# Hybrid decoder layer on one core: gate and up products share seven PSUM accumulators, and the stage is emitted in modelled order

## The chip, the cores and the metric

The kernel runs on one core of one Trainium2 chip. The metric is the device time of one execution in microseconds (us). Traces come from one profiled execution each.

## The reference

One decoder layer on 256 tokens, all in float32, width D = 2048, hidden width D_FF = 5632. Cut to what matters here:

```python
h = rms_norm(x, g_mix); z = h @ w_in            # 2048 x 17424, feeds three token mixers
x = x + merged @ w_o                            # merged: gated sum of the mixers' outputs
h = rms_norm(x, g_ffn)
gate, up = split(h @ w_gate_up, 2, axis=-1)     # 2048 x 11264
x = x + (silu(gate) * up) @ w_down              # 5632 x 2048
x = x + (p @ w_ple) * sigmoid(rms_norm(x, g_ple) @ w_ple_gate)
return rms_norm(x, g_final)
```

The result has to be float32-accurate. The change lies in the line that makes `gate` and `up`.

## The kernel before

**A product.** The 256 tokens are two halves of 128, called h = 0 and 1. The activations, transposed, are the stationary operand (128 features by 128 tokens); a weight tile (128 features, "k tile", by 512 columns) streams past. Both operands are split into a high and a low part of type fp32r, and one product of a k tile with one half is three matmuls of 512 columns: high by high, high by low, low by high (`products`, rows L244, L245, L246). A block of 512 output columns has one PSUM accumulator (`acc`) per half.

**A weight.** Weights come in pairs of k tiles, 128x2x512 float32, 512 KB. SP issues the load into a tile `raw`; ScalarE (ACT) copies it to the high part `whi` (L110); VectorE (DVE) subtracts, `wlo = raw - whi` (L111). A pair is two L244-L246 products per half, 12 matmuls.

**The stages.** Mixers (w_in and three output projections), w_o in four blocks c = 0..3, the gate and up blocks, w_down, then the per-layer embedding (w_ple, w_ple_gate). D_FF is cut into eleven blocks j of 512. For each j there is a group of sixteen k tiles for gate (evacuated by `ev_gate`: ACT sigmoid, DVE multiply) and one for up (`ev_up`: DVE multiply, giving the tile `ga`), then `ga` is transposed on PE and split into the stationary `aT` for w_down. `CUT = 5`: gate and up for j = 0..4, a pass over w_down with what is there, gate and up for j = 5..10, a second pass. Each pass adds its four blocks into the residual `xr` (`ev_down`, two DVE adds of 128x512 per block).

**The order.** `run(plan)` cuts the groups into chunks of four k tiles and emits them in turn: loads up to three chunks ahead (`PREF_DMA = 2`), splits up to two (`PREF_SPLIT = 2`), transposes two chunks after their evacuation (`LAG = 2`). Five buffers for raw tiles, five for split pairs, five PSUM banks for accumulators, three (`misc`) for transposes. These pools are open for the whole kernel, so the first gate weights are loaded and split while w_o's matmuls still run. The normalised input of gate and up is made per block c of xr after w_o: transposes, then `scaled_split` by g_ffn (`next_stat`, tiles `xhi`, `xlo`). The tokens' norms (`rn`) are applied in the evacuation.

**The end.** The last group is the last 256 columns of w_ple_gate, kind "hold": its split weights are kept in SBUF (`whold`), half 0 of the tokens is multiplied with all sixteen k tiles first, then half 1, and `ev_last` (sigmoid `pgs`, L965, final norm, output) of half 0 runs under the matmuls of half 1.

Of the kernel before, what the change touches and what calls it, by code (L numbers as in the profile page):

```python
# [19 lines left out]
P = 128  # L20
# [20 lines left out]
class Group:  # L41
# [6 lines left out]
    def __init__(self, w, kts, c0, n, stat, evac, need=(), pre=None, kind="tok", cost=1.3):  # L48
        self.w, self.kts, self.c0, self.n = w, list(kts), c0, n
        self.stat, self.evac, self.need, self.pre, self.kind = stat, evac, need, pre, kind  # L50
        self.cost = cost
        self.ps = None
        self.held = []


class Chunk:
    def __init__(self, g, ks, first, last):
        self.g, self.ks, self.first, self.last = g, ks, first, last
        self.raw = None
        self.parts = None  # L60


@with_exitstack
def kernel(
# [80 lines left out]
    junk = const.tile([P, NB], F32, name="junk")
    siga0 = const.tile([P, 2, 248], F32, name="siga0")
# [32 lines left out]
    def split_w(c):  # L179
# [70 lines left out]
    def run(plan):  # L250
# [3 lines left out]
        while now[0] < len(chunks):  # L254
# [12 lines left out]
            if c.first:  # L267
                for name in g.need:
                    finish(name)
                g.ps = [  # L270
                    acc.tile([P, NB], F32, tag="acc", name=nm("acc")) for _ in range(2)
# [547 lines left out]
    run(plan)  # L819
# [20 lines left out]
    xr2 = [big(f"xr{c}", (P, 2, 1024)) for c in range(2)]  # L840
    xr = [col(xr2, c) for c in range(4)]
    xT = {"f": [], "p": []}
# [10 lines left out]

    def ev_wo(c):
        def f(g, i):
# [3 lines left out]
            defer(i, lambda: next_stat("f", c, "g_ffn"))  # L859
# [3 lines left out]
    for c in range(4):  # L863
        nc.gpsimd.dma_start(out=xr[c], in_=x_v[:, :, c * NB : (c + 1) * NB])
    gfb = big("gfb", (P, D))
    nc.gpsimd.dma_start(out=gfb, in_=g_final.partition_broadcast(P))
    plan = [Group(w_o_v, ks16, c * NB, NB, blk(mT), ev_wo(c)) for c in range(4)]


# [5 lines left out]
    def ev_gate(j):  # L875
        def f(g, i):
            m = med("ga")
            for h in range(2):
                act.activation(out=m[:, h, :], in_=g.ps[h], func=AF.Sigmoid, scale=rr("f", h))
                stt(m[:, h, :], g.ps[h], rr("f", h), m[:, h, :], ALU.mult, ALU.mult)  # L880
            gt[j] = m
# [3 lines left out]
    def ev_up(j):  # L885
        def f(g, i):
            m = gt[j]
            for h in range(2):
                stt(m[:, h, :], g.ps[h], rr("f", h), m[:, h, :], ALU.mult, ALU.mult)

            def later():
                a = big("aT", (P, 2, 4, T), F32R)
                aT[j] = (a[:, 0, :, :], a[:, 1, :, :])
                to_stat(m, *aT[j])

            defer(i, later)

        return f

    def ev_down(c, final):  # L900
        def f(g, i):
            for h in range(2):
                tt(xr[c][:, h, :], xr[c][:, h, :], g.ps[h], ALU.add)
            if final:
                stats_add("p", c, xr[c])
                defer(i, lambda: next_stat("p", c, "g_ple"))
# [4 lines left out]
    CUT = 5  # L911
    for lo, hi in ((0, CUT), (CUT, NJ)):
        for j in range(lo, hi):
            plan.append(Group(w_gu_v, ks16, j * NB, NB, x_stat("f"), ev_gate(j)))
            plan.append(Group(w_gu_v, ks16, NJ * NB + j * NB, NB, x_stat("f"), ev_up(j)))
        for c in range(4):
            plan.append(Group(w_dn_v, range(4 * lo, 4 * hi), c * NB, NB, blk(aT), ev_down(c, hi == NJ)))
# [4 lines left out]
    def prep_p():  # L922
# [4 lines left out]
        split(pT["hi"], pT["lo"], pt)  # L927

    def ev_ple(c):
        def f(g, i):  # L930
            m = med("ple")
            for h in range(2):
                act.activation(out=m[:, h, :], in_=g.ps[h], func=AF.Copy)
            pl[c] = m
# [3 lines left out]
    def pg_half(ps, c, h, a, n, slot):  # L938
# [8 lines left out]
        tt(xh, xh, gfb[:, c * NB + a : c * NB + a + n], ALU.mult)  # L947
# [108 lines left out]
```

## Time and profile before

| | |
|---|---|
| median of 3 runs | 1902.97 us (1901.8 to 1903.25) |
| the profiled execution | 1903.29 us, its span 1901.4 us |
| PE busy | 1884.7 us (99%), 8688 matmuls and transposes |
| DVE busy | 1187.9 us (62%), 1409 instructions |
| ACT busy | 927.1 us (49%), 1067 instructions |
| POOL busy | 9.1 us, 22 instructions |
| memory | 359.58 MB read, 190 GB/s over the span |
| mean clock of PE | 0.998 |

Busy shares are means over stages with different limits. An engine that is not the last to be waited for has idle time that costs nothing; the rows of waits and the chain of work that ended last tell which engine that is. In such rows `wlo<-raw,whi` is an instruction that writes the tile wlo from raw and whi, L111 its line, `<-ACT whi L110` what released it.

### The profile page before, as it was taken

How to read it: one execution, taken by the hardware profiler on the slowest of the kernel's cores; microseconds unless marked ns; L12 is line 12 of the kernel's file. 1: busy time of each engine (PE TensorE's matmuls, PEld its weight loads, DVE VectorE, ACT ScalarE, POOL GpSimd, SP SyncE). 2: the span in 40 equal slices, each digit the busy share in tenths (PEclk: the TensorE clock that was granted, in tenths of full speed). 3: DMA queues.
4: the chain of work that ended last, by engine and by line, in shares of the span. 5: the costliest groups of instructions: out<-in, count | busy, mean ns of one | idle time of the engine just before them, and what ended most of it. 6: DMA issues, size and time to landing. Idle time of an engine off the chain costs nothing.

```text
span 1901.4 us, 22742 instructions
## 1 busy us (share of the span) xinstructions
PE 1884.7 (99%) x8688; PEld 1570.9 (83%) x8688; DVE 1187.9 (62%) x1409; ACT 927.1 (49%) x1067; POOL 9.1 (0%) x22
## 2 busy tenths in 40 slices
PE   8999999999999999999999999999999999999998
PEld 7888888888888888888888888888888888888887
DVE  6457777668889888645555555554545555555555
ACT  6656556554444435644445544443344444444554
POOL 0000000000000000000000000000000000000000
PEclk9999999999999999999999999999999999999999
DMA  8766556556666656676655666665666666655553
GB/s 309 237 182 185 174 178 189 173 150 176 197 182 196 192 154 220 190 242 189 209 189 187 186 191 189 189 189 190 196 190 190 196 191 190 188 188 189 183 183 122
DMA packets 190254, 363.18 MB, mean 191 GB/s; under 512 B 11600, under 2 KB 20432, under 8 KB 189760
## 3 DMA queue, kind: packets, MB, share of 16 engines
q1 hardware_dynamic: 189248, 358.12, 61.6%
q0 software_dynamic: 896, 3.61, 0.6%
q8 instruction: 68, 1.11, 0.2%
q14 instruction: 42, 0.34, 0.1%
HBM read 359.58 MB, written 2.10 MB: 190 GB/s over the span
## 4 chain that ended last, share of the span: by engine, by line
PE 98%; DVE 1%; DMA 0%; ACT 0%; SPq 0%; issue 0%; DVEq 0%
PE acc L246 32%; PE acc L245 32%; PE acc L244 32%; PE tr L313 2%; PE sc L522 1%; DMA x<-in_x_feat_dram 0%; DVE rw L688 0%; DVE wlo L111 0%; PE ov L593 0%; PE ov L594 0%; PE ov L592 0%; ACT whi L110 0%; PE sc L549 0%; SPq L165 0%; SPq L164 0%; ACT hhi L321 0%
## 5 line engine op out<-in xcount | busy, mean ns | idle before, releaser
L111 DVE TENSOR_TENSOR wlo<-raw,whi 128x1024 fp32r<-128x1024 f32 (+2 forms) x678 | 813.2, 1202 | 673.6 <-ACT whi L110 672.3
L110 ACT ACTIVATE whi<-raw 128x1024 fp32r<-128x1024 f32 (+2 forms) x678 | 706.0, 1043 | 903.7 <-PE acc L246 832.3
L244 PE MATMUL acc<-whi,hhi 128*128 128x512 f32 (+1 forms) x1120 | 433.1, 387 | 5.2 <-ACT whi L110 5.1
L245 PE MATMUL acc<-wlo,hhi 128*128 128x512 f32 (+1 forms) x1120 | 430.3, 384 | 0.5 <-DVE wlo L111 0.5
L246 PE MATMUL acc<-whi,hlo 128*128 128x512 f32 (+1 forms) x1120 | 430.6, 384 | 0.0
L244 PE MATMUL acc<-whi,xhi 128*128 128x512 f32 (+1 forms) x832 | 321.4, 386 | 0.0
L246 PE MATMUL acc<-whi,xlo 128*128 128x512 f32 (+1 forms) x832 | 320.6, 385 | 0.0
L245 PE MATMUL acc<-wlo,xhi 128*128 128x512 f32 (+1 forms) x832 | 320.3, 385 | 0.0
L244 PEld LDWEIGHTS acc<-whi,hhi 128*128 128x128 f32 x1120 | 210.9, 188 | 46.2 <-ACT whi L110 5.6
L245 PEld LDWEIGHTS acc<-wlo,hhi 128*128 128x128 f32 x1120 | 210.9, 188 | 42.2 <-DVE wlo L111 1.4
L246 PEld LDWEIGHTS acc<-whi,hlo 128*128 128x128 f32 x1120 | 210.8, 188 | 41.8
L246 PEld LDWEIGHTS acc<-whi,xlo 128*128 128x128 f32 x832 | 156.3, 188 | 31.5
L244 PEld LDWEIGHTS acc<-whi,xhi 128*128 128x128 f32 x832 | 156.3, 188 | 30.9
L245 PEld LDWEIGHTS acc<-wlo,xhi 128*128 128x128 f32 x832 | 156.4, 188 | 30.8
L244 PE MATMUL acc<-whi,aT 128*128 128x512 f32 x352 | 137.5, 391 | 0.0
L246 PE MATMUL acc<-whi,aT 128*128 128x512 f32 x352 | 137.1, 389 | 0.0
L245 PE MATMUL acc<-wlo,aT 128*128 128x512 f32 x352 | 136.9, 389 | 0.0
L104 DVE SCALAR_TENSOR_TENSOR cv<-uT,vec,cv 128x255 f32<-128x255 f32 (+15 forms) x240 | 110.8, 466 | 4.8
L246 PEld LDWEIGHTS acc<-whi,aT 128*128 128x128 f32 x352 | 66.1, 188 | 13.8
L245 PEld LDWEIGHTS acc<-wlo,aT 128*128 128x128 f32 x352 | 66.1, 188 | 13.6
L244 PEld LDWEIGHTS acc<-whi,aT 128*128 128x128 f32 x352 | 66.1, 188 | 13.6
L244 PE MATMUL acc<-whi,mT 128*128 128x512 f32 x128 | 50.2, 392 | 0.0
(250 smaller groups left out, 1369.1 us busy)
## 6 DMA issues: line engine op xcount, KB each, us to landing
raw<-in_w_in_dram SPq DMA_DIRECT2D x262, 512.0 KB, 3.7
raw<-in_w_gate_up_dram SPq DMA_DIRECT2D x176, 512.0 KB, 3.7
raw<-in_w_down_dram SPq DMA_DIRECT2D x88, 512.0 KB, 4.1
raw<-in_w_gla_out_dram SPq DMA_DIRECT2D x32, 512.0 KB, 3.7
raw<-in_w_o_dram SPq DMA_DIRECT2D x32, 512.0 KB, 3.6
raw<-in_w_ple_gate_dram SPq DMA_DIRECT2D x24, 512.0 KB, 4.4
raw<-in_w_sc_out_dram SPq DMA_DIRECT2D x16, 512.0 KB, 4.3
raw<-in_w_cf_out_dram SPq DMA_DIRECT2D x16, 512.0 KB, 4.3
```

The costliest lines, as they stand in the source:

```text
L104: dve.scalar_tensor_tensor(out=o, in0=a, scalar=s, in1=b, op0=op0, op1=op1)
L110: a = act.activation(out=hi, in_=src, func=AF.Copy)
L111: b = dve.tensor_tensor(out=lo, in0=src, in1=hi.bitcast(F32), op=ALU.subtract)
L244: pe.matmul(o, lhsT=shi[:, hs], rhs=whi, start=st, stop=False)
L245: pe.matmul(o, lhsT=shi[:, hs], rhs=wlo, start=False, stop=False)
L246: pe.matmul(o, lhsT=slo[:, hs], rhs=whi, start=False, stop=sp)
L313: pe.transpose(b[:, q, h * P : h * P + P], src[:, h, (j + q) * P : (j + q) * P + P], ident,)
L522: pe.matmul(b[:, e, :], lhsT=K[:, dt, :], rhs=Q[:, dt, :], start=q == 0, stop=q == 1)
```

## The change

**Seven products instead of eight.** Gate block j and up block j are one `Quad`: per pair of k tiles a 2 by 2 by 2 block product (two halves of tokens, two k tiles, two blocks), eight products. `PAIRS = "soosooso"` names the eight pairs of k tiles. In an "s" pair (0, 3, 6) seven products of sums replace the eight: seven stationary operands are combinations of the four blocks of the input (`quad_stat`, tile `st`), and seven moving operands are taken from four pieces of weights: gate, up with gate's first k tile added in place, a sum tile (`sum`), and one more k tile. DVE makes them with four additions of 128x512; three pieces are split in full, one half. The seven go to PSUM banks 7, 6, 1, 2, 5, 3, 4.

**Eight products with five differences.** In an "o" pair there are eight products (24 matmuls) into banks 2, 4, 5, 3, which needs six stationary combinations. Gate's piece is split as before. For up's piece ACT writes `whi` and then `wlo = -whi`, and a DMA issued by POOL with `accum_op=add` adds the weight from HBM onto it. There are 55 of these accumulating DMAs, 512 KB each.

**Combining.** `quad_mid` and `quad_end` form the four outputs from the seven banks: per quad one ACT copy, seven DVE additions or subtractions with PSUM, four `stt` and two sigmoids; before there were two sigmoids per j and four multiplications.

**The order.** From gate and up to the end a class `Flow` emits the instructions: it keeps a model of when ACT, DVE and PE are free and puts splits, evacuations and transposes between the products by it. Loads are issued one by one while fewer than `RAWS = 4` raw tiles live, `PARTS = 7` split pairs. PSUM: seven banks for accumulators, one (`misc`) for transposes.

**Pools and passes.** The mixers and w_o are one plan in the old `run`. Then the pools for raw tiles, split pairs, t4 and PSUM are closed and opened with the new sizes. w_down has three passes, after j = 0..3, 4..7, 8..10. `whold` is one tile per pair of k tiles.

Where the order of instructions moves, in three places. First PE at the end of w_o. Before (`mT` is w_o's stationary, `xhi` and `xlo` that of gate and up), the last row of w_o and the first of gate:

```order
L244 MATMUL acc_8109<-whi_8198,mT_7642 128x512
L245 MATMUL acc_8109<-wlo_8199,mT_7642 128x512
L246 MATMUL acc_8109<-whi_8198,mT_7642 128x512
L244 MATMUL acc_8290<-whi_8230,xhi_7808 128x512
L245 MATMUL acc_8290<-wlo_8231,xhi_7808 128x512
L246 MATMUL acc_8290<-whi_8230,xlo_7809 128x512
```

After, at the same place (L639 to L641 are the old `products`, L236 to L238 the new `three`, `tr` a transpose, `st` the combined stationary; in brackets the semaphores that an instruction waits for):

```order
L640 MATMUL acc_8126<-wlo_8216,mT_7643 128x512
L641 MATMUL acc_8126<-whi_8215,mT_7643 128x512
L1276 MATMUL tr_8318<-ident,xr_1331_7602 128x128 [waits DMASW6_49,DVE_49]
L1276 MATMUL tr_8318<-ident,xr_1331_7602 128x128 [waits DVE_49]
L1276 MATMUL tr_8318<-ident,xr_1331_7602 128x128 x2
L236 MATMUL acc_8363<-whi_8325,st_7815 128x512 [waits DMAHW2_49,DMAHW1_49,DMAHW3_49,DMAHW0_49,DMAHW4_49,DMASW2_49,DMAHW5_49,DMASW1_49,DMAHW6_49,DMASW0_49,DMAHW7_49,Activation_49,Pool_49]
L236 MATMUL acc_8380<-whi_8325,st_7815 128x512
L237 MATMUL acc_8363<-wlo_8326,st_7815 128x512 [waits DVE_49]
```

The products follow w_o directly before and need two tiles that were split in w_o's time; now four transposes and tiles of the new pools stand in between.

Second, ACT at the same place. Before, whi_8198 is w_o's last split:

```order
L110 ACTIVATE whi_8198<-raw_8136 128x1024 [waits DMAHW7_49,PE_49]
L110 ACTIVATE whi_8230<-raw_8190 128x1024 [waits DMAHW0_49,PE_49]
L110 ACTIVATE whi_8234<-raw_8192 128x1024 [waits DMAHW1_49,PE_49]
L110 ACTIVATE whi_8282<-raw_8226 128x1024 [waits DMAHW2_49,PE_49,Activation_49]
L110 ACTIVATE whi_8286<-raw_8228 128x1024 [waits DMAHW3_49,PE_49,Activation_49]
L830 ACTIVATE junk,ssq_7755<-xr_1309_7569 128x512 [waits DMASW6_49,DVE_49]
```

After, whi_8215 is w_o's last split (L505 is the old `split`, L209 and L213 those of `split_ops`, L1224 the squares for the norm, L1260 the scaling of `quad_stat`):

```order
L505 ACTIVATE whi_8215<-raw_8153 128x1024 [waits DMAHW7_49,PE_49]
L209 ACTIVATE whi_8325<-raw_8312 128x1024 [waits DMAHW1_49,DVE_49,PE_49]
L1224 ACTIVATE junk,ssq_7756<-xr_1331_7602 128x512 [waits DMASW6_49,DVE_49]
L209 ACTIVATE whi_8331<-raw_8310 128x1024 [waits DMAHW0_49]
L1224 ACTIVATE junk,ssq_7756<-xr_1331_7602 128x512 [waits DVE_49,Activation_49]
L209 ACTIVATE whi_8338<-sum_8323 128x1024
L209 ACTIVATE whi_8346<-raw_8312 128x512 [waits DVE_49]
L696 ACT_TABLE_LOAD
L696 ACTIVATE s_8275<-v_8273 128x2 [waits DVE_49]
L1260 ACTIVATE sz_8349<-tr_8318,vec 128x2x128 [waits PE_49]
L1260 ACTIVATE sz_8349<-tr_8318,vec 128x256
L209 ACTIVATE whi_8370<-raw_8314 128x1024 [waits DMAHW2_49]
```

The splits for gate stood ahead of the squares of w_o's last block and now stand among them, and the first one's tile lies where a tile of w_o's closed pool lay: it waits for the last matmul of w_o (PE_49).

Third, PE at the end, in the hold group. Before (acc_14203 is half 0, acc_14204 half 1; rows left out in between are more of the same k tiles), where the one half passes into the other:

```order
L244 MATMUL acc_14203<-whold_14238,xhi_13241 128x256
L245 MATMUL acc_14203<-whold_14238,xhi_13241 128x256
L246 MATMUL acc_14203<-whold_14238,xlo_13242 128x256
L244 MATMUL acc_14204<-whold_14149,xhi_12759 128x256
L245 MATMUL acc_14204<-whold_14149,xhi_12759 128x256
L246 MATMUL acc_14204<-whold_14149,xlo_12760 128x256
```

After (acc_14808 is half 0, acc_14873 half 1; whold_14769 is the last of eight pairs of k tiles, whold_14742 the fifth):

```order
L236 MATMUL acc_14873<-whold_14742,xhi_13955 128x256
L236 MATMUL acc_14808<-whold_14769,xhi_13955 128x256 [waits Activation_49]
L237 MATMUL acc_14873<-whold_14742,xhi_13955 128x256
L238 MATMUL acc_14873<-whold_14742,xlo_13956 128x256
...
L237 MATMUL acc_14808<-whold_14769,xhi_13955 128x256 [waits DVE_49]
L238 MATMUL acc_14808<-whold_14769,xlo_13956 128x256
...
L238 MATMUL acc_14873<-whold_14742,xlo_13956 128x256
L236 MATMUL acc_14873<-whold_14751,xhi_13955 128x256
```

Half 1 starts before half 0 is through, and half 0 ends 19 matmuls ahead of the end where it ended 48 ahead of it.

The diff, cut to what is spoken of here:

```diff
+    def split_ops(self, piece, t, src, deps=(), load=None, frees=(), cost=1.2, sl=slice(0, 2), neg=None):
...
+        a = self._op("A", cost * 0.88, lambda: nc.scalar.activation(out=hi(), in_=src(), func=AF.Copy), deps, load, piece,
+                     frees if neg else ())
+        if neg:
+            def go():
+                nc.scalar.activation(out=lo(), in_=hi().bitcast(F32), func=AF.Copy, scale=-1.0)
+                nc.gpsimd.dma_start(out=lo(), in_=neg, accum_op=ALU.add)
...
+    BANKS = "6712453"
...
+    def add_quad(self, g):
...
+            r1, r2 = (Load(g.w, 2 * p, c, NB) for c in g.cs)
+            if kind == "s":
...
+                        self.nc.vector.tensor_tensor(out=X(0), in0=R2(0), in1=R2(1), op=ALU.add),
...
+                b1 = self.split_ops(pc[0], 0, lambda r=r1: r.raw, load=r1)
+                t1 = self.add_op(lambda R2=R2: R2(0), lambda R2=R2: R2(0), lambda R1=R1: R1(0), [t3], r1)
+                t2 = self.add_op(lambda X=X: X(1), lambda R2=R2: R2(0), lambda R2=R2: R2(1), [t1], r1)
+                self.split_ops(pc[1], 0, lambda r=r2: r.raw, [t1], r2, [r2])
+                t4 = self.add_op(lambda R1=R1: R1(0), lambda R1=R1: R1(1), lambda X=X: X(1), [t2, b1], r1)
+                self.split_ops(pc[2], 0, lambda x=x: x[0], [t2], None, [])
+                self.split_ops(pc[3], 0, lambda r=r1: r.raw[:, 0:1, :], [t4], r1, [r1], 0.65, slice(0, 1))
+                terms = [("7", 3, 2, 0), ("6", 5, 2, 1), ("1", 0, 0, 0), ("2", 1, 0, 1), ("5", 4, 1, 0), ("3", 6, 1, 1), ("4", 2, 3, 0)]
...
+                self.split_ops(pc[1], 0, lambda r=r2: r.raw, load=r2, frees=[r2],
+                               neg=g.w[:, 2 * p : 2 * p + 2, g.cs[1] : g.cs[1] + NB])
+                self.split_ops(pc[0], 0, lambda r=r1: r.raw, load=r1, frees=[r1])
+                for part, (z, slot, i) in enumerate((("2", 0, 0), ("4", 2, 0), ("5", 2, 1), ("3", 4, 1))):
...
+    PAIRS = "soosooso"
+    def quad_stat(p, b, z):
+        st = big("st", (P, 2, 8, P), F32R)
...
+            act.activation(out=o, in_=v[:, q, :, :], func=AF.Copy, scale=v1("g_ffn", 2 * p + q))
+        if PAIRS[p] == "s":
+            n = 7
+            tt(z[:, 3, :], z[:, 7, :], z[:, 0, :], ALU.subtract)
+            tt(z[:, 4, :], z[:, 7, :], z[:, 2, :], ALU.subtract)
+            tt(z[:, 5, :], z[:, 0, :], z[:, 4, :], ALU.subtract)
+            tt(z[:, 6, :], z[:, 1, :], z[:, 5, :], ALU.subtract)
+        else:
+            n = 6
+            tt(z[:, 4:6, :], z[:, 0:2, :], z[:, 2:4, :], ALU.subtract)
+        split(st[:, 0, :n, :], st[:, 1, :n, :], z[:, :n, :])
...
+    run(plan)
+    for d in deferred:
+        d[1]()
+    phase.close()
+    phase = open_pools(raws=(4,), sums=(1,), wparts=(7,), t4=(3,), at=(1,), acc=(1, PSUM), misc=(1, PSUM))
...
+    def quad_mid(g, ps):
+        g.v, g.m = v, m = med("vx"), med("ga")
+        return [
+            flow.op("A", 0.6, lambda: act.activation(out=m[:, 0, :], in_=ps["1"], func=AF.Copy)),
+            flow.op("D", 0.7, lambda: tt(v[:, 0, :], ps["6"], m[:, 0, :], ALU.subtract)),
+            flow.op("D", 0.7, lambda: tt(v[:, 1, :], v[:, 0, :], ps["7"], ALU.add)),
+        ]
...
-    CUT = 5
-    for lo, hi in ((0, CUT), (CUT, NJ)):
+    for lo, hi in ((0, 4), (4, 8), (8, NJ)):
         for j in range(lo, hi):
-            plan.append(Group(w_gu_v, ks16, j * NB, NB, x_stat("f"), ev_gate(j)))
-            plan.append(Group(w_gu_v, ks16, NJ * NB + j * NB, NB, x_stat("f"), ev_up(j)))
+            plan.append(Quad(w_gu_v, j * NB, (NJ + j) * NB, PAIRS, quad_mid, quad_end(j)))
...
-    run(plan)
+    flow.run(plan)
```

More of the change, by code (lines that the diff above doesn't have):

```diff
@@ L60, in __init__ @@
         self.parts = None
+class Quad:
+    def __init__(self, w, c0, c1, pairs, mid, end):
+        self.w, self.cs, self.pairs, self.mid, self.end = w, (c0, c1), pairs, mid, end
+        self.ps = {}
+class Op:
+    def __init__(self, eng, cost, fn, deps=()):
+        self.eng, self.cost, self.fn, self.deps = eng, cost, fn, list(deps)
+        self.end = None
+class Load:
+    def __init__(self, w, k, c0, n):
+        self.w, self.k, self.c0, self.n = w, k, c0, n
+        self.raw, self.freed = None, False
@@ L86, in nm, with open_pools @@
         return f"{s}_{uid[0]}"
+    pools = {}
+    def open_pools(**sizes):
+        stack = ExitStack()
+        for name, (bufs, *space) in sizes.items():
+            kw = dict(space=PSUM) if space else {}
+            pools[name] = stack.enter_context(tc.tile_pool(name=nm(name), bufs=bufs, **kw))
+        return stack
+    phase = open_pools(
+        gla=(1,), raws=(5,), wparts=(5,), t4=(5,), acc=(5, PSUM), misc=(3, PSUM)
+    )
     def big(name, shape=(P, 8, T), dt=F32):
@@ L270, in run @@
                 g.ps = [
-                    acc.tile([P, NB], F32, tag="acc", name=nm("acc")) for _ in range(2)
+                    pools["acc"].tile([P, NB], F32, tag="acc", name=nm("acc")) for _ in range(2)
                 ]
@@ L873, in rr @@
         return rn[key][:, h : h + 1]
[L875 to L881, printed above, removed]
-        return f
[L885 to L892, printed above, removed]
-                aT[j] = (a[:, 0, :, :], a[:, 1, :, :])
-                to_stat(m, *aT[j])
-            defer(i, later)
-        return f
+    flow = Flow(nc, tc, pools, nm, big, split, quad_parts=lambda p: fst[p])
@@ new lines, in a_stat, with pe_part, rest, x_part @@
+    def a_stat(j, m, z):
+        def pe_part(b):
+            if z == 0:
+                a = pools["at"].tile([P, 2, 4, T], F32R, tag="at", name=nm("aT")) if j % 4 == 3 else big("aT", (P, 2, 4, T), F32R)
+                aT[j] = (a[:, 0, :, :], a[:, 1, :, :])
+            four(b, m, z)
+        def rest(b):
+            split(aT[j][0][:, z : z + 2, :], aT[j][1][:, z : z + 2, :], b)
+        return pe_part, rest, 0.8, ("a", 2 * j + z // 2)
+    def x_part(c, j):
+        def pe_part(b):
+            four(b, xr[c], j)
+        def rest(b):
+            quad_stat(2 * c + j // 2, b, med("sz", (P, 8, P)))
+        return pe_part, rest, 2.0, ("f", 2 * c + j // 2)
@@ L900, in ev_down, with p_part, pe_part, rest @@
+    def p_part(c, j):
+        def pe_part(b):
+            if c % 2 == 0 and j == 0:
+                xT["p"].append((big("xhi", dt=F32R), big("xlo", dt=F32R)))
+            four(b, xr[c], j)
+        def rest(b):
+            hi, lo = xT["p"][-1]
+            for q in range(2):
+                a = (c % 2) * 4 + j + q
+                scaled_split(hi[:, a, :], lo[:, a, :], b[:, q, :], v1("g_ple", 4 * c + j + q))
+        return pe_part, rest, 1.0, ("p", 2 * c + j // 2)
     def ev_down(c, final):
-        def f(g, i):
-            for h in range(2):
-                tt(xr[c][:, h, :], xr[c][:, h, :], g.ps[h], ALU.add)
+        def f(g, ps):
+            def add(h):
+                tt(xr[c][:, h, :], xr[c][:, h, :], ps[h], ALU.add)
+            ops = [flow.op("D", 0.7, lambda h=h: add(h)) for h in range(2)]
```

449 lines of the change are left out of this document (391 added, 58 removed).

## The prediction, made before the changed kernel ran

> **What bounds the kernel now.** First the page's busy times and the chain of work that ended last, then the waits of PE over the whole span.
>
> ```profile
> PE 1884.7 (99%) x8688; PEld 1570.9 (83%) x8688; DVE 1187.9 (62%) x1409; ACT 927.1 (49%) x1067; POOL 9.1 (0%) x22
> PE 98%; DVE 1%; DMA 0%; ACT 0%; SPq 0%; issue 0%; DVEq 0%
> ```
>
> ```profile
> PE acc L244 <- ACT whi L110: 5.1, 1, 5.1
> PE mu L690 <- DVE rw L688: 1.7, 1, 1.7
> PE acc L245 <- DVE wlo L111: 0.5, 1, 0.5
> ```
>
> PE is 98% of the chain, and its waits add up to 7.3 us, one at the start and two in the mixers. So behind w_o PE never waits: what is taken from its queue there is gained in full, and what makes it wait there is lost in full. Now the stage of gate and up, from the groups of a stretch that holds the end of w_o and gate and up blocks; the windows below give the shares of a stretch of gate and up alone (columns: wall; busy us of PE, PEld, DVE, ACT, POOL; clock; DMA share; GB/s).
>
> ```profile
> L111 DVE TENSOR_TENSOR wlo<-raw,whi 128x1024 fp32r<-128x1024 f32 x77 | 94.4, 1225 | 96.2 <-ACT whi L110 96.1
> L110 ACT ACTIVATE whi<-raw 128x1024 fp32r<-128x1024 f32 x77 | 81.7, 1061 | 112.2 <-PE acc L246 112.2
> L104 DVE SCALAR_TENSOR_TENSOR ga<-acc,y,ga 128x512 f32<-128x512 f32 x16 | 11.3, 746 | 2.1 <-ACT ga L879 2.1
> L879 ACT ACTIVATE ga<-acc,y 128x512 f32<-128x512 f32 x9 | 6.1, 689 | 3.9 <-PE acc L246 3.9
> L111 DVE TENSOR_TENSOR aT<-tr,aT 128x512 fp32r<-128x512 f32 x8 | 5.1, 681 | 0.0
> L110 ACT ACTIVATE aT<-tr 128x512 fp32r<-128x512 f32 x8 | 4.3, 585 | 0.0
> L313 PE MATMUL tr<-ident,ga 128*128 128x128 f32 x32 | 4.1, 272 | 0.0
> ```
>
> ```profile
> 30.00:40.00 10.00, 10.00 (x46) 8.29 (x45) 3.97 (x5) 7.47 (x8) 0.00 (x0) 1.00 1.03 387
> 1046.00:1160.00 114.00, 114.00 (x516) 94.57 (x516) 62.61 (x68) 54.02 (x62) 0.00 (x0) 1.00 0.65 189
> ```
>
> ACT waits for PE (a buffer comes free), DVE for ACT: both have room, and DMA at 189 GB/s is well below the 387 GB/s that it reaches when full. DVE is at 55% there, ACT at 47%.
>
> **The change, step by step.** The base is the profiled execution, 1903.29 us, 0.3 us above the median of the runs (1902.97), which changes nothing at this size.
>
> 1. Matmuls. Per quad three "s" pairs take 21 matmuls instead of 24: 9 fewer, times 11 quads 99; the order of PE's instructions shows that the rest stays (8344 rows to 8245). What one costs is the spacing in the stream:
>
> ```profile
> 1319.77 0.39 PE L244 MATMUL acc<-whi,aT 128*128 128x512 f32 x1
> 1363.97 0.39 PE L244 MATMUL acc<-whi,aT 128*128 128x512 f32 x1
> ```
>
> 195 matmuls lie between these starts: 44.20/195 = 0.2267 us. Gain 99 x 0.2267 = **22.4 us**, and no more, whatever the other engines do.
>
> 2. Does a quad stay bound by PE? PE: 8 x 24 - 9 = 183 matmuls, 41.5 us. Further rows for 128x512 tiles and for the small steps:
>
> ```profile
> L101 DVE TENSOR_TENSOR xr<-xr,acc 128x512 f32<-128x512 f32 x2 | 1.3, 679 | 0.0
> L111 DVE TENSOR_TENSOR wlo<-raw,whi 128x512 fp32r<-128x512 f32 x12 | 8.2, 690 | 7.9 <-ACT whi L110 7.7
> L321 ACT ACTIVATE xhi<-tr,vec 128x256 fp32r<-128x256 f32 x6 | 2.6, 471 | 1.9 <-DVE xlo L104 1.9
> L301 ACT ACT_TABLE_LOAD x1 | 1.3, 1283 | 0.0
> L830 ACT ACTIVATE junk<-xr 128x512 f32<-128x512 f32 x2 | 1.2, 623 | 0.0
> L830 ACT ACTIVATION_READ_ACCUMULATOR junk<-xr 128x1 f32 x2 | 0.4, 185 | 0.0
> ```
>
> DVE per quad: "s" pairs 3 x (3 full subtractions x 1.225 + 0.690 + 4 additions x 0.68) = 21.3; "o" pairs 5 x 1.225 = 6.1; seven PSUM combinations x 0.68 = 4.8; four multiplications x 0.746 = 3.0; two splits of aT x 0.68 = 1.4. Sum 36.5 of 41.5 us, 88%. ACT: "s" 3 x (3 x 1.061 + 0.63) = 11.4; "o" 5 x 3 x 1.061 = 15.9; evacuation and aT 3.2. Sum 30.5, 73%. So PE stays the longest, but DVE's slack falls from some 45% to 12%. What hides all these additions is PE's own queue of products; the cover on DVE is 5.0 us per quad.
>
> 3. The accumulating DMAs, five of 512 KB per quad. The trace has no accumulating transfer. The nearest rows are the POOL queue's loads (KB, us to landing) beside SP's:
>
> ```profile
> raw<-in_w_gate_up_dram SPq DMA_DIRECT2D x176, 512.0 KB, 3.7
> xr<-in_x_dram POOLq DMA_DIRECT2D x4, 512.0 KB, 7.5
> gfb<-in_g_final_dram POOLq DMA_DIRECT2D x1, 1024.0 KB, 5.3
> pt<-in_p_feat_dram POOLq DMA_DIRECT2D x1, 256.0 KB, 3.3
> L864 POOL DMA_DIRECT2D xr<-in_x_dram x4: 722/730/762, 836.0 to 838.2; - x4
> ```
>
> Latency: four xr loads issued within 2.2 us took 7.5 us each; 256 KB alone 3.3, 1 MB alone 5.3. I take 4.5 (a plain 512 KB lies near 4, and reading what is there comes on top), ends 3.3 and 9.5 (7.5 and 2 for the second read). In mid-quad the negation is emitted some 13 us (58 to 60 matmuls) ahead of the product that reads it, of which two ACT passes take 2.1: 11 us are there, and a landing of up to 9.5 is hidden. POOL does nothing else in this stage, so its queue holds up nobody. Throughput: 512 KB at 387 GB/s is 1.35 us; with k the cost of an accumulating byte relative to a plain one a quad needs 16 x 1.35 + 5 x 1.35 k = 21.7 + 6.8 k: 28.5 us at k = 1, 35.2 at 2, 42 at 3. I take k between 1 and 2: one read more per byte written; cost nothing. The Trainium skill ("Collectives: The Full Stack", "The bandwidth ceiling: the fold count and why AG ≠ RS ≠ AR") has reduce-scatter at 32.35 GB/s against 62.28 for all-gather, since an add reads two sources, a ratio of 1.93. An estimate from that figure puts a quad's DMA at 35 us, under PE's 41.5, and the sum stays; no run here shows it.
>
> 4. The border of w_o and the first quad. Before, two splits of gate were ready when w_o ended and there was no wait. Now the new pools lie over the old ones: SP's first load waits for DVE's last w_o split, and ACT's first split for w_o's last matmul. By hand from that matmul, in ACT's order: split 1.06, two squares with read-outs 1.6, two splits 2.1 (4.8), DVE's half split behind them ends at 6.7; ACT goes on with a half split 0.63, table load 1.28, root 0.2, two scaled copies 0.94 (7.9), two splits of the first "o" pair (10.0), split of st about 0.95, negation 1.06 (12.0), accumulating DMA 4.5 (16.5), then ten matmuls, 2.3: 18.8. PE's work up to there is 45 matmuls (10.2) and 8 transposes at 4.1/32 (1.0), 11.2. Loss **7.5 us**; with the ends of the landing, 6.3 and 12.5. A gain is excluded: nothing waits there now.
>
> The longest single idle of PE in that chain is from 13.5 to 16.5, 3 us. How the clock (the column before the last two) takes idle time, the end of the trace shows, where the last matmul is at 1892:
>
> ```profile
> 1892.00:1895.00 3.00, 0.14 (x2) 0.00 (x0) 2.15 (x8) 2.16 (x4) 0.00 (x0) 0.98 0.62 209
> 1895.00:1898.00 3.00, 0.00 (x0) 0.00 (x0) 1.68 (x5) 0.72 (x1) 0.00 (x0) 0.50 0.48 178
> ```
>
> It falls to 0.50 about 3 us after the last matmul, so a landing over about 5 us would also bring slow matmuls here. The Trainium skill ("TensorE: Matmul & The Clock Gate", "Part 1: The HAM clock gate") has a window of about 3.4 us of idle before the half clock and as long busy before the full one; the trace agrees with the first. By it an estimate of 1.7 us would come on top, and the forecast would be 1895.
>
> 5. The tail. In the hold group half 0 ended 48 matmuls of 256 columns before the end, now 19.
>
> ```profile
> 1886.42 0.47 ACT L965 ACTIVATE pgs<-acc,y 128x256 f32<-128x256 f32 x1 [1.88 <-PE acc L246]
> 1890.19 0.71 ACT L988 ACTIVATE xr<-xr,fr 128x512 f32<-128x512 f32 x1
> 1892.18 0.47 ACT L965 ACTIVATE pgs<-acc,y 128x256 f32<-128x256 f32 x1 [1.28 <-PE acc L246]
> ```
>
> The two evacuations start 5.76 us apart, 0.12 per matmul; ACT is done with half 0 after 4.48 us (1890.90). With 19 x 0.12 = 2.3 us the second starts 2.2 us late. And the last three pairs' whold reuse buffers that half 1 frees only then: two or three short waits, 0.6 in all (between 0 and 2). Together **+2.8** (0 to 5).
>
> 6. The single transpose bank. A block's second four transposes wait until DVE has split the first. Before there were three banks. By hand both arrive within about a microsecond, so 0 to 1.5 us per quad; I take 0.2, nearest to "arrives in time", **+2** (0 to 16).
>
> 7. Free: the third pass over w_down (8 more additions of 0.68 on DVE, under 16 k tiles of products each), the residual's transposes moved into quads, the late load of gfb (5.3 us, needed a whole group later).
>
> Sum: 1903.29 - 22.4 + 7.5 + 2.8 + 2 = **1893** us.
>
> **The rivals.**
>
> *VectorE loses its lead.* At 88%, with additions in place that need one another (sum, then gate into up, then the next sum), the order decides. Before, DVE waited 96.2/77 = 1.25 us for ACT per split; in the chain of an "s" pair ACT and DVE take turns four times. If PE waits 0.6 us per quad more, 6.6 in all, two thirds of what is left of the gain are gone, at 0.95 us per quad all of it; at 1.9 us the time is 1914. For it: 12% of slack where there were 45. Against: seven buffers of split pairs instead of five let DVE run ahead, and by my hand chain an "s" pair's last split is ready 4 to 5 us before PE reads it. Time 1899 to 1914.
>
> *The accumulating DMAs fill the queues* (the slower side). The place is every quad's five accumulations; from k = 2.9 DMA needs as long as PE (21.7 + 19.8), and from k = 3.2 the remaining gain of 10 us is gone (0.95 per quad). At k = 4 a quad takes 48.8, 11 x 7.3 = 80 us more: 1973. For it: POOL's loads took 7.5 where SP's took 3.7, and there is no row of an accumulation. Against: that was with four at once beside SP's.
>
> *The border and the tail are hidden.* If splits and landing come early enough, items 4 to 6 shrink to 3: 1884. Against: the order shows PE's first product waiting for a split that waits for PE.
>
> That the products are not saved is excluded by the order.
>
> **How the numbers follow.** A measurement tells about 0.2%, 3.8 us, from no change: "same" is 1899.2 to 1906.8. Main case 1885 to 1899, 0.58; hidden border 0.08; VectorE 0.19, about half of it within "same", half slower; DMA 0.13; 0.02 for others. Faster 0.67, same 0.11, slower 0.22. The range takes the first three, with items 4 to 6 at their ends (1903.3 - 22.4 + 3 = 1884 to 1914), and leaves out the DMA case: 1883 to 1914. The likeliest case's own range is 1885 to 1899.
>
> **What would show it.** Right: the spacing of matmuls unchanged at 0.227; in the first 20 us behind w_o PE waits for ACT, DVE and a POOL transfer, 6 to 12 us in all; in later quads PE's waits below 0.5 us each, DVE near 88%, ACT near 73%; an accumulating DMA lands in 4 to 7 us; the two pgs stand 4.5 us apart. Wrong: waits of PE for wlo in each quad (VectorE), or a DMA share near 1.0 and raw tiles that ACT waits for (DMA), or landings over 11 us, which would turn up as a wait of PE for the queue of POOL in each "o" pair.

## The result: 1958.65 us, 2.95% slower, and the profile after

The changed kernel takes 1958.65 us (median of four runs, 1955.82 to 1962.88) against 1903.07 (four runs, 1901.8 to 1903.25); the ratio is 1.0295, interval 1.0271 to 1.032. The profiled execution has a span of 1954.1 us, 52.7 more than before. From the page of the changed kernel: busy times, the queues, the chain of work that ended last, the accumulating DMAs.

```profile
PE 1892.1 (97%) x8589; PEld 1553.9 (80%) x8589; DVE 1310.5 (67%) x1646; ACT 1041.1 (53%) x1207; POOL 75.3 (4%) x77
q0 software_dynamic: 15856, 32.44, 9.1%
PE 75%; DVE 10%; DMA 9%; issue 3%; ACT 2%; DVEq 0%; POOL 0%; SPq 0%; ACTq 0%; POOLq 0%
raw<-in_w_gate_up_dram SPq DMA_DIRECT2D x176, 512.0 KB, 4.6
wlo<-in_w_gate_up_dram POOLq DMA_DIRECT2D x55, 512.0 KB, 8.0
```

The 99 matmuls are gone (8688 records to 8589), yet the chain, 98% PE before, is 75% PE: a fifth of the span now runs through DVE and DMA. The waits of PE, and those for a raw weight tile on the two engines that make its parts (engine, waiting tile and line, releaser: us, times, longest). L236 to L238 are the three matmuls of a product; vx and ga are the tiles into which DVE combines the banks:

```profile
PE acc L236 <- DVE vx L496: 17.0, 15, 1.8
PE acc L237 <- DMA wlo<-in_w_gate_up_dram: 8.1, 1, 8.1
PE tr L1276 <- DVE aT L506: 6.0, 8, 1.6
PE tr L1276 <- DVE ga L499: 5.7, 3, 2.3
...
PE acc L237 <- DVE wlo L220: 4.2, 6, 1.5
```

```profile
ACT whi L209 <- DMA raw<-in_w_gate_up_dram: 82.5, 27, 4.9
DVE raw L228 <- DMA raw<-in_w_gate_up_dram: 65.8, 23, 4.8
DVE sum L266 <- DMA raw<-in_w_gate_up_dram: 40.4, 20, 3.9
```

The last three groups are new: in this stage of the kernel before, ACT's splits waited for PE alone. PE's waits name DVE, and DVE and ACT wait for loads. The timeline of DVE and then PE in the first quad of the second pass shows how the one becomes the other (start, length, instruction, idle before it):

```profile
1386.57 0.69 DVE L266 TENSOR_TENSOR sum<-raw 128x512 f32<-128x512 f32 x1 [2.14 <-DMA raw<-in_w_gate_up_dram]
1391.09 0.69 DVE L228 TENSOR_TENSOR raw<-raw,raw 128x512 f32<-128x512 f32 x1 [3.83 <-DMA raw<-in_w_gate_up_dram]
...
1397.69 0.68 DVE L220 TENSOR_TENSOR wlo<-raw,whi 128x512 fp32r<-128x512 f32 x1
1398.29 0.68 DVE L496 TENSOR_TENSOR vx<-acc,ga 128x512 f32<-128x512 f32 x1
...
1403.27 1.27 DVE L496 TENSOR_TENSOR vx<-vx,acc 128x512 f32<-128x512 f32 x2
```

```profile
1393.69 0.50 PE L237 MATMUL acc<-wlo,st 128*128 128x512 f32 x1 [1.49 <-DVE wlo L220]
1399.84 0.47 PE L236 MATMUL acc<-whi,st 128*128 128x512 f32 x1 [0.60 <-DVE vx L496]
1404.60 0.50 PE L236 MATMUL acc<-whi,st 128*128 128x512 f32 x1 [1.75 <-DVE vx L496]
```

DVE stands still for 2.1 and 3.8 us until a raw tile lands, then runs without a gap, and the combinations of this quad, behind the late splits in its queue, come too late for PE, which needs their banks again. The windows of the same stage (columns: wall; busy us of PE, PEld, DVE, ACT, POOL; clock; DMA share; GB/s) show a DMA share of 0.88 and a clock that drops where PE has stood:

```profile
1086.80:1093.60 6.80, 3.82 (x9) 3.05 (x10) 4.21 (x6) 1.69 (x2) 0.00 (x0) 0.50 0.99 260
1274.60:1278.00 3.40, 3.40 (x11) 2.63 (x10) 2.13 (x3) 1.54 (x2) 0.00 (x0) 0.50 0.76 251
1400.00:1440.00 40.00, 36.93 (x165) 29.80 (x165) 26.40 (x35) 23.25 (x26) 4.84 (x4) 1.00 0.88 238
```

And a part that nobody had touched is longer. The last matmul of w_o, before and after:

```profile
1059.66 0.39 PE L246 MATMUL acc<-whi,mT 128*128 128x512 f32 x1
```

```profile
1068.54 0.40 PE L641 MATMUL acc<-whi,mT 128*128 128x512 f32 x1
```

PE's order up to there is the same row for row, and so are its waits (5.2 against 5.1 us at the start, 1.7 in the mixers). A stretch of 60 us in the mixers holds fewer matmuls (PE busy and its count, clock, DMA share, GB/s; before, then after):

```profile
640.00:700.00 60.00, 60.00 (x266) 1.00 0.59 181
```

```profile
640.00:700.00 60.00, 60.00 (x264) 1.00 0.60 187
```

The starts there are 0.2289 us apart (95 between 630.333 and 652.077) where they were 0.2267.

Split by the starts of PE's matmuls, the 52.7 us of span are: 8.9 up to the end of w_o; 41.0 from there to the last product of w_down (731.98 us before, 772.97 now), in which the 99 matmuls save 22.4 and PE's gaps over the normal spacing grow from 0.7 to 64.1; 2.75 in the rest. Of the 64.1, 14.1 lie at the border of w_o (up to 1118 us) and 50 in the quads and passes behind it. PE's waits in this stage add up to 43 us; the rest is in gaps that the rows of waits do not count in full, and in matmuls at the half clock, some 7 us (an estimate: PE was busy for 14 us of the 17 in which the clock stood at 0.50).

### The profile page after: what moved, and what is told of

Its sections match the earlier page's. It is cut to its first block, busy times and chain, and to the rows that moved or that the text cites. A ratio compares the mean times of both kernels' runs of the same rounds, so it can differ in the third digit from the quotient of the medians.

```text
span 1954.1 us, 23164 instructions
## 1 busy us (share of the span) xinstructions
PE 1892.1 (97%) x8589; PEld 1553.9 (80%) x8589; DVE 1310.5 (67%) x1646; ACT 1041.1 (53%) x1207; POOL 75.3 (4%) x77
## 4 chain that ended last, share of the span: by engine, by line
PE 75%; DVE 10%; DMA 9%; issue 3%; ACT 2%; DVEq 0%; POOL 0%; SPq 0%; ACTq 0%; POOLq 0%
PE acc L639 17%; PE acc L641 17%; PE acc L640 17%; DMA raw<-in_w_gate_up_dram 7%; PE acc L237 7%; PE acc L238 7%; PE acc L236 7%; DVE wlo L220 6%; ACT whi L209 2%; DVE raw L228 1%; PE tr L708 1%; PE tr L1276 1%; DVE vx L496 1%; DMA raw<-in_w_down_dram 1%; PE sc L917 1%
## 5 line engine op out<-in xcount | busy, mean ns | idle before, releaser
L506 DVE TENSOR_TENSOR wlo<-raw,whi 128x1024 fp32r<-128x1024 f32 (+2 forms) x378 | 450.0, 1195 | 301.6 <-ACT whi L505 300.7
L505 ACT ACTIVATE whi<-raw 128x1024 fp32r<-128x1024 f32 (+2 forms) x378 | 390.7, 1036 | 472.4 <-PE acc L641 438.0
L209 ACT ACTIVATE whi<-raw 128x1024 fp32r<-128x1024 f32 (+1 forms) x333 | 329.2, 1003 | 314.4 <-PE acc L238 170.7
L639 PE MATMUL acc<-whi,hhi 128*128 128x512 f32 (+1 forms) x1120 | 436.8, 390 | 5.2 <-ACT whi L505 5.2
L220 DVE TENSOR_TENSOR wlo<-raw,whi 128x1024 fp32r<-128x1024 f32 (+1 forms) x278 | 315.8, 1142 | 180.7 <-ACT whi L209 180.4
L641 PE MATMUL acc<-whi,hlo 128*128 128x512 f32 (+1 forms) x1120 | 433.3, 387 | 0.0
L236 PE MATMUL acc<-whi,st 128*128 128x512 f32 x671 | 265.4, 397 | 16.2 <-DVE vx L496 15.9
L237 PE MATMUL acc<-wlo,st 128*128 128x512 f32 x671 | 263.9, 393 | 12.4 <-DMA wlo<-in_w_gate_up_dram 8.1
L238 PE MATMUL acc<-whi,st 128*128 128x512 f32 x671 | 261.5, 392 | 0.0
L639 PEld LDWEIGHTS acc<-whi,hhi 128*128 128x128 f32 x1120 | 211.2, 189 | 46.2 <-ACT whi L505 5.2
L641 PEld LDWEIGHTS acc<-whi,hlo 128*128 128x128 f32 x1120 | 211.0, 188 | 45.1
L236 PEld LDWEIGHTS acc<-whi,st 128*128 128x128 f32 x671 | 126.4, 189 | 50.3 <-DVE vx L496 17.2
L237 PEld LDWEIGHTS acc<-wlo,st 128*128 128x128 f32 x671 | 127.0, 189 | 41.6 <-DMA wlo<-in_w_gate_up_dram 8.9
L238 PEld LDWEIGHTS acc<-whi,st 128*128 128x128 f32 x671 | 127.0, 189 | 26.6
L236 PE MATMUL acc<-whi,aT 128*128 128x512 f32 x352 | 138.9, 395 | 2.8 <-DVE ga L496 1.7
L238 PE MATMUL acc<-whi,aT 128*128 128x512 f32 x352 | 138.5, 393 | 0.0
L214 POOL DMA_DIRECT2D wlo<-in_w_gate_up_dram x55 | 66.2, 1204 | 845.6 <-ACT wlo L213 833.9
L236 PEld LDWEIGHTS acc<-whi,aT 128*128 128x128 f32 x352 | 66.6, 189 | 17.2 <-DVE ga L496 2.1
```

Of the source, the lines that this page charges most:

```text
L209: a = self._op("A", cost * 0.88, lambda: nc.scalar.activation(out=hi(), in_=src(), func=AF.Copy), deps, load, piece, frees if neg else ())
L214: nc.gpsimd.dma_start(out=lo(), in_=neg, accum_op=ALU.add)
L220: lambda: nc.vector.tensor_tensor(out=lo(), in0=src(), in1=hi().bitcast(F32), op=ALU.subtract),
L236: pe.matmul(o, lhsT=s[0], rhs=w[0], start=start, stop=False)
L237: pe.matmul(o, lhsT=s[0], rhs=w[1], start=False, stop=False)
L238: pe.matmul(o, lhsT=s[1], rhs=w[0], start=False, stop=stop)
```

## The experiments

Theory B says that the accumulating DMAs make the loads late; theory C that the seven banks, the one transpose bank and DVE's work do it alone; theory A that the mixers are slower because their weight tiles lie elsewhere in SBUF.

**e1_align**, where the tiles lie, first try.

```diff
-    siga0 = pools["gla"].tile([P, 2, 248], F32, name="siga0")
+    siga0 = pools["gla"].tile([P, 2, 256], F32, name="siga0")[:, :, :248]
```

> One tile of the pool gla is 64 bytes longer, so that the split weight tiles of the mixers and w_o begin at a multiple of 128 bytes again; nothing else changes. Theory A (alignment: in the changed kernel these tiles begin at 64 modulo 128, and matmuls that read them start 0.2289 us apart instead of 0.2267): the end of w_o comes at 1060 us instead of 1068.5, the time falls by 8.9 us to 1950. Rival (the slow stretch belongs to that execution or chip, or to the new order of pools in another way): no change, 1958.

1971.69 us (ratio 1.0368, 1.0344 to 1.0392): the wrong way. The mixers were slower still, 260 matmuls in the same 60 us, and w_o's last matmul started at 1083.58. So 64 bytes in one tile move the end of a part that is bound by PE by 15 us; place matters, but it is not the multiple of 128.

**e5_same_offset**, second try.

```diff
+    siga0 = pools["gla"].tile([P, 2, 400], F32, name="siga0")[:, :, :248]
```

> One tile of the pool gla is 1216 bytes longer, so that the split weight tiles of the mixers begin at 1536 modulo 2048, as the stationary tiles of t8 do (before, both began at 896; in the changed kernel at 320 against 1536; with 64 bytes more at 384 against 1536, where the matmuls stood 0.2324 us apart). Theory A2 (matmuls of 512 columns are slower where moving and stationary tile differ in that offset): spacing 0.2267 and the end of w_o at 1060 us, 8.9 earlier; time about 1950. Rival A3 (the spacing depends on something else of the new order of pools): between 0.2280 and 0.2330, 1955 to 1975.

1938.97 us (1.0196, 1.0179 to 1.0213). The mixers are back to the old pace:

```profile
640.00:700.00 60.00, 60.00 (x266) 1.00 0.56 180
```

```profile
1059.17 0.39 PE L641 MATMUL acc<-whi,mT 128*128 128x512 f32 x1
```

Theory A2's number for the end of w_o held. The time fell by more than the 8.9 us of that part; the rest, some 11 us, lies in the quads (772.97 us to 761.5), where nothing was changed and the kernel's own runs differ by up to 7. By the addresses of the built program the operands of the quads lie at 1536 and 1536 modulo 2048 in both kernels, and the spacing there is 0.227 in both; what made the 11 us stays open.

**e2_no_accumulate** and **e3_plain_copy**, the DMAs themselves.

```diff
-                nc.gpsimd.dma_start(out=lo(), in_=neg, accum_op=ALU.add)
```

> Leaves out the 55 accumulating DMAs (the low part of up's weights in the pairs with eight products is then only minus the high part); ACT's negation and all else stay. Theory B (the accumulating DMAs make the loads of raw weights late, and DVE's queue, which holds the additions for the next pair ahead of the evacuations, passes that on to PE): the 10 us at the border of w_o go and most of the 45 us of waits in the quads, time 1905 to 1920; waits for raw fall from 184 us to under 40. Rival C (DVE's work, the seven banks without a second set and the one transpose bank make the waits by themselves): only the border goes, 1945 to 1950.

```diff
-                nc.gpsimd.dma_start(out=lo(), in_=neg, accum_op=ALU.add)
+                nc.gpsimd.dma_start(out=lo(), in_=neg)
```

> The 55 DMAs stay at their place and size, but copy the weight over the tile instead of adding it (the low part is then the weight itself). Theory B1 (it is the read of the destination and the addition that cost): nearly as without the DMAs, 1910 to 1925, landing about 4 us. Theory B2 (any further 512 KB per pair on the software queue does it): 1950 to 1960, landing 6 to 8 us. Rival C: 1945 to 1960 whatever the landing is.

Without the DMAs 1906.48 us (1.0017, 1.0008 to 1.0026), with plain copies 1924.66 (1.0111, 1.0096 to 1.0126). Neither computes the right layer: e2 leaves the weight out of up's low parts, e3 puts the whole weight there. Theory C falls: with the same banks, the same transposes and the same work on DVE the 52 us are gone, and PE waits for vx 0.9 us where it waited 17.0. From e2, PE's wait and a window (columns as in the windows above):

```profile
PE acc L235 <- DVE vx L495: 0.9, 1, 0.9
```

```profile
1400.00:1440.00 40.00, 40.00 (x180) 32.64 (x180) 30.74 (x40) 28.57 (x32) 0.00 (x0) 1.00 0.65 205
```

In numbers the DMAs cost 52 us, of which 18 remain when they only copy and 34 belong to the accumulation. Waits for raw fell to 87 us in e2, not under 40 as expected: idle time of DVE and ACT is not lost to PE one for one. The queue of the plain copies and their landing, 5.5 us where about 4 was expected:

```profile
q0 software_dynamic: 15856, 32.44, 5.5%
wlo<-in_w_gate_up_dram POOLq DMA_DIRECT2D x55, 512.0 KB, 5.5
```

The same bytes take 9.1% of the 16 engines' span when added and 5.5% when copied. Less the 0.6% of the queue's other loads that is 3.0 us of 16 engines for one accumulation and 1.7 for one copy, k = 1.8.

**e4_dma_in_model**, whether the order of DVE's queue does it.

```diff
     def start_of(self, op):
-        return max([self.clk[op.eng]] + [d.end for d in op.deps])
+        z = getattr(op, "load", None)
+        return max([self.clk[op.eng], z.at if z else 0.0] + [d.end for d in op.deps])
...
+            z.at = max(self.clk.values()) + 3.5
             self.live_raw.append(z)
```

> The model that sets the order learns that a load takes 3.5 us, so that an operation on a tile that is not there yet no longer stands ahead of an evacuation; the work is the same. Theory B with the queue order as its second half: waits of PE for vx and ga on DVE shrink by half or more, 1935 to 1945. Rival (late loads hold the splits up anyway, whatever the order): within 5 us of 1958.

1954.73 us (1.0268, 1.0252 to 1.0283): the rival. With loads as late as this, the other order is worth 4 us. It reckons with 3.5 us for every load, where the landings in the changed kernel reach 10.5; an order made for longer ones was not tried.

**e6_six_raw**, loads issued earlier (and one split pair fewer).

```diff
-    RAWS, PARTS = 4, 7
+    RAWS, PARTS = 6, 6
...
-    phase = open_pools(raws=(4,), sums=(1,), wparts=(7,), t4=(3,), at=(1,), acc=(1, PSUM), misc=(1, PSUM))
+    phase = open_pools(raws=(6,), sums=(1,), wparts=(6,), t4=(3,), at=(1,), acc=(1, PSUM), misc=(1, PSUM))
```

> Six raw tiles and six split pairs instead of four and seven, so that loads are issued up to two tiles earlier; the accumulating DMAs stay. Theory B (loads come late because four tiles don't cover a landing that contention has lengthened): waits for raw fall from 184 us to under 80, PE's waits in the quads by two thirds, 1920 to 1935. Rival D (the 16 DMA engines are near full at 0.87 to 0.91, more loads in flight only lengthen every landing): raw lands in 6 us or more instead of 4.8, time within 10 us of 1958.

1922.57 us (1.0109, 1.0094 to 1.0124), 36 us less than the changed kernel, with all accumulating DMAs in place. PE's waits and the waits for raw:

```profile
PE acc L237 <- DMA wlo<-in_w_gate_up_dram: 12.9, 18, 1.8
...
PE acc L237 <- DVE wlo L220: 4.8, 4, 3.9
```

```profile
DVE sum L266 <- DMA raw<-in_w_gate_up_dram: 48.9, 24, 4.0
...
DVE raw L228 <- DMA raw<-in_w_gate_up_dram: 22.1, 14, 3.4
```

ACT, which waited 82.5 us for raw tiles, does not wait for them any more, and PE's waits for vx are gone. Theory B holds in its main part: four raw tiles did not cover the landing. Rival D was right that the landings of raw would lengthen (median 5.6 us in the first pass, 4.8 with four), but two tiles more outweigh it. What is left is new: PE now waits for the accumulating DMAs directly, 18 times.

**e7_dve_subtracts** and **e8_two_seven**, without accumulating DMAs and with the full result.

```diff
-                self.split_ops(pc[1], 0, lambda r=r2: r.raw, load=r2, frees=[r2],
-                               neg=g.w[:, 2 * p : 2 * p + 2, g.cs[1] : g.cs[1] + NB])
+                self.split_ops(pc[1], 0, lambda r=r2: r.raw, load=r2, frees=[r2])
```

> In the pairs with eight products DVE subtracts up's high part as it does for gate; no negation and no accumulating DMA. DVE gets five subtractions of 1.22 us per quad more, ACT five passes of 1.06 less. Without the DMAs DVE was busy 31 of 40 us. Theory B: 31 + 5.9 = 37 of 40, PE is still ahead, 1905 to 1915. Rival E (DVE has no room, and the evacuations behind its subtractions hold PE): 1920 to 1950.

```diff
-    PAIRS = "soosooso"
+    PAIRS = "sooosooo"
```

> As e7_dve_subtracts, with two of eight pairs in seven products (sooosooo) instead of three. 33 more matmuls than with three, 7.5 us; DVE per quad loses about 6 us of work. If DVE is what limits with three (rival E), this one is the faster: 1905 to 1912. If PE limits (theory B), it is 7.5 us slower than e7_dve_subtracts: 1913 to 1922.

1911.83 us (1.0051, 1.0036 to 1.0066) and 1907.0 (1.0021, 1.0011 to 1.003). With three pairs DVE is busy 37 of 40 us and PE still waits for it (4.4 us for ga, 3.3 for vx), with two it is busy 32 to 33 of 40; rival E seemed to hold. Both still had four raw tiles and the slow mixers.

**e9_three_dve_six**, **e10_two_dve_six**, **e11_two_hold**: e7 and e8 with the six raw tiles of e6 and the offset of e5, and the last group as before.

> Three seven-product pairs, all low parts by DVE (as e7_dve_subtracts), six raw tiles and six split pairs, and the tile of gla 1216 bytes longer (as e5_same_offset). Theory B: of e7's 1911.8 the offset takes 9 and earlier loads most of the remaining 17 us of PE's waits behind w_o: 1890 to 1898. Rival E (DVE, busy 37 of 40 us, is the limit whatever the loads do): 1900 to 1905.

> As e9_three_dve_six with two seven-product pairs. e8's 1907.0 less 9 for the offset and up to 4 of its 8 us of waits: 1894 to 1898; if theory B holds for e9 this one is 5 to 7.5 us slower than e9, if rival E holds it is faster by 3 or more.

```diff
...
-                        pc.tile.append(self.big("whold", (P, 2, 2, n), F32R))
-                    return pc.tile[0]
+                        pc.tile.append(self.big("whold", (P, 2, 4, n), F32R))
+                    return pc.tile[0][:, :, off : off + 2, :]
```

> As e10_two_dve_six, and the last group holds four k tiles per tile again, so that half 0 of the tokens is through before half 1 begins, 48 matmuls ahead of the end instead of 19. The prediction's tail term: 2.8 us faster than e10. Rival (the tail of the changed kernel is long for another reason): within 0.5 us of e10.

1891.06 us (0.994, 0.9927 to 0.9954), 1896.93 (0.997, 0.9958 to 0.9981) and 1894.38 (0.9957, 0.9945 to 0.997). With three pairs the kernel is now 5.9 us faster than with two, so e7 was held by loads and not by DVE's work: rival E falls. A window of e9 (columns as in the windows above) has DVE at 92% and PE without a gap:

```profile
1400.00:1440.00 40.00, 40.00 (x181) 32.78 (x180) 36.96 (x46) 22.00 (x25) 0.00 (x0) 1.00 0.67 197
```

The hold group is worth 2.55 us. The two evacuations of half 0 and half 1 in e10, then in e11:

```profile
1881.75 0.48 ACT L1478 ACTIVATE pgs<-acc,y 128x256 f32<-128x256 f32 x1 [1.67 <-PE acc L238]
...
1886.13 0.45 ACT L1478 ACTIVATE pgs<-acc,y 128x256 f32<-128x256 f32 x1
```

```profile
1877.94 0.47 ACT L1480 ACTIVATE pgs<-acc,y 128x256 f32<-128x256 f32 x1 [3.05 <-PE acc L238]
...
1883.70 0.47 ACT L1480 ACTIVATE pgs<-acc,y 128x256 f32<-128x256 f32 x1 [1.27 <-PE acc L238]
```

In e10 the second waits for ACT (no releaser stands behind it), in e11 for PE.

**e12_accumulate_six**: the accumulating DMAs with everything else mended, none at the border.

```diff
...
-                               neg=g.w[:, 2 * p : 2 * p + 2, g.cs[1] : g.cs[1] + NB])
+                               neg=None if p == 1 and g.cs[0] == 0 else g.w[:, 2 * p : 2 * p + 2, g.cs[1] : g.cs[1] + NB])
```

> The changed kernel with accumulating DMAs, six raw tiles, six split pairs and the offset, and DVE's subtraction in the first quad's first pair with eight products alone (so that no accumulating DMA stands at the border of w_o). e6's 1922.6 less 9 for the offset and 6 to 10 for the border: 1904 to 1908. If landings of 8 us hold PE in every pair also here, 15 us of waits for them stay and nothing is won at the border: 1912 to 1916.

1913.35 us (1.0059, 1.0047 to 1.0072), the second case. 12.4 us of waits for the DMAs stay, and at the border a wait of 3.9 us (e6, for DVE's wlo) only gives way to one of 3.8 for the DMA of the next such pair:

```profile
PE acc L237 <- DMA wlo<-in_w_gate_up_dram: 12.4, 15, 3.8
```

**e14_two_accumulate** and **e13_three_dve_six_hold**: load or latency, and the version that the runs point to. e13 is e9 with e11's hold group; e14 is e13 with the DMAs kept in pairs 2 and 5.

```diff
...
-                               neg=g.w[:, 2 * p : 2 * p + 2, g.cs[1] : g.cs[1] + NB])
+                               neg=g.w[:, 2 * p : 2 * p + 2, g.cs[1] : g.cs[1] + NB] if p in (2, 5) else None)
```

> As e13, but two of a quad's five pairs with eight products (pairs 2 and 5) keep the negation and the accumulating DMA: 22 DMAs instead of 55, none at the border of w_o. Theory F (five per quad load the 16 DMA engines to 0.9, and the queueing makes both landings long): DMA share near 0.77, landing 6 to 7 us, PE's waits behind the border under 3 us, 1887 to 1891. Rival G (an accumulating DMA is too slow for its place by itself, about 8 us at any load): 0.3 us of wait for each as in e12, 22 x 0.3 = 6 us, 1894 to 1898.

> The version that the runs point to: three seven-product pairs, low parts by DVE, six raw tiles, the offset, and the hold group of e11. e9's 1891.06 less the 2.55 us that e11 gained on e10: 1888.5.

e14 took 1898.17 us (0.9979, 0.997 to 0.9988). The DMA share in the quads is 0.71 to 0.79, and the landing is still 7.1 us:

```profile
wlo<-in_w_gate_up_dram POOLq DMA_DIRECT2D x22, 512.0 KB, 7.1
```

```profile
PE acc L237 <- DMA wlo<-in_w_gate_up_dram: 4.5, 5, 2.5
```

Less load takes one microsecond off the landing. The plain copies of e3 landed in 5.5 us at a share of 0.77 to 0.84, so the greater part of what is left over a copy goes with the accumulation itself. Rival G is nearer by the time, but not by the waits: PE waits for five of the 22, and 2.5 of the 4.5 us are one wait 21 us behind w_o; behind that it is 2.0, under theory F's 3 us. Between the two the run does not decide. e13 took 1888.44 us (0.9923, 0.991 to 0.9935), as expected to 0.1 us: 14.5 us faster than before.

## Why the prediction was wrong

It gave 1893 us, 1883 to 1914, and 0.22 for slower. Its steps in turn:

1. *99 matmuls, 22.4 us*: held. In the stage the spacing is 0.227, and e13, where the rest is mended, is 14.5 us faster overall.

2. *DVE per quad 36.5 of 41.5 us, covered by PE's queue*: the work was put somewhat too high, 88% where e2 has 31 of 40 us, 78%; the sum counts each row at full length, and in the timeline above instructions of 0.68 us start 0.60 apart (1397.69 and 1398.29). The cover held as far as work goes: in e9 DVE is at 92% and PE has no gap. What was not counted is DVE's waits. DVE stood still for 106 us behind loads, 9.7 per quad where 5.0 were free. That sum alone does not decide, since DVE still stood 70 us in e2; there ACT, which makes the high parts first, waited 16.6 us for raw tiles and not 82.5.

3. *The accumulating DMAs, "cost nothing"*: the step that failed, and it cost 52 us (e2). k came out as taken: 1.8, between 1 and 2. The Trainium skill's ratio of 1.93 ("Collectives: The Full Stack", "The bandwidth ceiling: the fold count and why AG ≠ RS ≠ AR") is near the 1.8, so the trace agrees. The price of a plain load was too low: the step took 1.35 us, the time at 387 GB/s, so 21.7 us for sixteen loads. But the window from 1046 us that the prediction shows has a share of 0.65 at only 189 GB/s, and e9, with the sixteen loads alone, has 0.64 to 0.67, 27 us of 41.5. With five times 3.0 us that is 42 us by the engines' busy time (an estimate; the step's sum at k = 1.8 is 34), so nothing was free; measured is a share of 0.88 over quads that take longer.

   The step asked two questions, whether the engines have the time and whether the accumulation lands before its reader, and answered both with yes. The third was missing: what such a share does to the other loads on the same engines. Their landing went from 3.7 to 4.6 us median, and from at most 5.0 up to 10.5, while the change had cut the raw tiles from five to four and holds those of a seven-product pair through four additions. e6 shows that this is the larger part: two more tiles bring back 36 us. The second answer failed too: the landing of the accumulation, 8.0 us, was under the upper end of 9.5, but the 11 us of lead were not there. In e6, where loads are earlier, the landings reach 10.6 us at most, and PE waits for 18 of the 55.

4. *The border, 7.5 us (6.3 to 12.5)*: 14.1. ACT's chain was right to a microsecond: the first negation ended 11.1 us behind the start of w_o's last matmul, against 12, and the accumulation was issued at 1079.91. But it landed after 9.8 us, not 4.5. That the clock would then halve was said for a landing over 5 us, and it did, for 6.8 us (first window above). Shorter idle times were enough too: behind waits of 1.8, 2.3 and 2.2 us the clock stood at 0.50 for 3.4 us each time (from 1223.4, 1274.6 and 1551.0), while other waits of 1.8 us brought no drop. The Trainium skill ("TensorE: Matmul & The Clock Gate", "Part 1: The HAM clock gate") has windows of about 3.4 us and the half clock after an idle one. The drops of 3.4 and 6.8 us agree with such windows; that a whole one has to be idle, these runs do not bear out. Without the DMAs the border costs 3.7 us (e9; 5.0 in e2, with four raw tiles).

5. *The tail, 2.8 us*: 2.75 in the spans, 2.55 by e11. The two evacuations stand 4.38 us apart; 4.5 was said.

6. *The single transpose bank, 2 us*: in e13, where loads are in time, PE waits 1.6 us for it in all. In e2, with the same bank and late loads but no DMAs, it is 1.2; so the 6.0 us here are DVE's lateness again.

A term was missing: 8.9 us in the mixers, since the new order of pools moved their tiles. That "the rest stays" was read from the order of instructions; it does not show addresses.

The rival on the slower side named these DMAs, and its times, up to 1973, hold the measured one; but it had 0.13, and the stated range left it out. Its path was a bound of bandwidth that needs k above 3.2 (its own sum gives 3.05 for 0.95 us per quad). Measured is k = 1.8, and e6 moves the same bytes 36 us faster; so a bound of bandwidth is not what cost the greater part, and that its times fit is luck. One of its signs was right: ACT waited 82.5 us for raw tiles, at a share of 0.88. And of the rival on VectorE it was the sign that was right (PE's waits name DVE), not the mechanism: DVE was not short of time but of weights.

## What to carry to other kernels

When a change adds transfers, ask after the share and the reader, and then after every other load on the same engines: how many tiles are in flight, how long each is held, and whether that covers a landing twice as long. PE's waits name the last link only: follow the named engine back to what it waited for itself, and make the experiment there. When pools are moved, compare the spacing of the untouched part first; it is a term of its own.

## What the hardware showed that was not expected

- Matmuls of 512 columns depend on where the two operands lie. By the addresses of the built programs, with stationary and moving tiles at 896 and 896 modulo 2048 bytes, or 1536 and 1536, they start 0.2267 us apart; with 1536 and 320 it is 0.2289, with 1536 and 384 0.2324. Over some 4,300 matmuls that is 9 to 24 us. Whether the difference of the two or the moving tile's own place counts was not tried.
- A DMA that adds 512 KB to SBUF lands after 8.0 us where the same copy needs 5.5, and takes 1.8 times the DMA engines' time; at a lower load (a DMA share of 0.71 to 0.79 instead of 0.85 to 0.91) it still takes 7.1.
